# A decoder trunk on one core: the unpaired matrices of the input projection are chained, and TensorE keeps the order in which the kernel is written

## The chip, the cores and the metric

The kernel runs on one core of a Trainium2 chip. The metric is the device time of one execution in microseconds (us). Three runs of the kernel before took 1710.2 to 1712.84 us, with a median of 1712.13 us. About 0.2% (some 3.5 us) is what a measurement of this kernel can tell from no change.

## The reference, cut to what matters

One layer of a hybrid decoder on 1024 tokens of width 2048, in float32:

```
h = rms_norm(x, norm_gain)
q, k, v, g_attn, xr, g_rec = split(h @ w_in)          # 2048 -> 4*1024 + 2*1024
q, k = rope(q), rope(k)                               # 8 heads, 2 maps of 64 each
o = diff_attention(q, k, v, lam)                      # causal, softmax(1) - lam*softmax(2)
o = rms_norm(o, subln_gain) * 0.8 * silu(g_attn)
r = rg_lru(causal_conv(xr, conv_w, conv_b), ...)      # 8 blocks of 128 channels
r = r * silu(g_rec)
out = rms_norm(x + concat(o, r) @ w_out, final_gain)
```

## The kernel before, in words

Every product of two float32 matrices is split: an operand becomes a rounded high part and a rest, and three matmuls of 128x512 (high x high, high x rest, rest x high) stand for one. The high part is a cast on ACT, the rest a subtraction on DVE or POOL (`split`, L189 and L190; L193 is the helper for all other two-operand elementwise work).

**The input projection** works on *pairs*: two column blocks of 128 of `w_in`, over one half of the depth (8 of 16 tiles of 128) and all 1024 tokens. A pair is one 2x2 block product by a Strassen scheme, so it needs 7 products, numbered `pi` = 0 to 6, instead of 8. A product is one *group* of 12 matmuls (4 depth tiles x 3 split parts) into one PSUM bank. The weight operand of a product is formed by `prep` from the pair's four raw loads (`x["11"]`, `"12"`, `"21"`, `"22"`): products 0, 1, 4 and 5 take one tile as it lies, product 2 needs two additions first, products 3 and 6 one. The token operands (`OPS`, seven of them) are the same for all pairs of a stretch.

Four banks serve a pair: `al` for products 0 and 3, `de` for 1, `be` for 2 and 5, `ga` for 4 and 6 (`BANKS`). Products 3, 5 and 6 do not begin a bank: they add to what lies there. Between two products of a bank `post` reads it:

- after product 0: ACT copies `al` to `a1` (L546)
- after product 1: DVE adds `de` to `a1`: result 11
- after product 3: ACT copies `al` to `u2` (L552), then DVE adds `be` and `u2` to `u3`. Product 5 may write `be` only when that is done
- after product 4: DVE adds `ga` and `u3`: result 22. Product 6 may write `ga` only then
- after products 5 and 6: DVE adds `be` and `u2` (result 21), `ga` and `u2` (result 12)

In the rows all these bank reads of DVE are `L193 b<-pp`. `pp_78`, `pp_79`, `pp_80` and `pp_81` of the order are `al`, `be`, `ga` and `de`.

The projection has three stretches: 8 pairs of recurrent columns over the first depth half; 24 pairs (16 attention, 8 recurrent) over the second; 16 attention pairs over the first. A recurrent pair of the second stretch spawns `recurrent` when it is done (convolution, gates, scan: work for DVE, ACT and POOL), an attention pair of the third `rope` or `values`. The first two pairs and the last two of a stretch are *dual*: their groups alternate, each pair with banks of its own (in the third only the first two). All others are *single*: products 0 to 6 of one pair, then 0 to 6 of the next. The list `q` of (pair, product) holds that order.

The loop over `q` runs, per step: raw loads ahead, `prep` of the step three places on (`LEAD`), the 12 matmuls with a tick of `sl` after each three, and `post`. Side work lives in generators that `sl` resumes at ticks, so it lands between groups.

**What sets the order on the engines.** What the loop emits is not the final order. A scheduler that works with a cost model of its own puts each engine's instructions in order when the kernel is built; the place in the program is the priority. On the chip every engine then runs its list in that fixed order.

**The rest.** `rec_half` does the recurrent half of the output projection (groups of 24 matmuls at L1079 to L1081) and feeds the attention between them: scores of a block of 128 queries into PSUM `sw` (L870, L871), mask and maximum on DVE (L875, L878), exponentials on ACT (L882), the weighted difference on DVE (L885 to L890, result `wide`), transposes on PE (L997), their split (L1006 on ACT, L1007 on DVE), product with the values (L1019 to L1022), and once per half head a norm (`head_out`, L968 and L979 on PE). `att_half` does the other half of the output projection and the last norm.

Of the kernel before, what the change touches and what calls it, by code (L numbers as in the profile page):

```python
# [121 lines left out]
class Trunk:  # L122
# [419 lines left out]
    def post(self, pr, pi):  # L542
# [16 lines left out]
        elif pi == 6:  # L559
            self.result(pr, "12", b["ga"], pr.u2)  # L560
            self.rel(pr.u2)
            if pr.done:
                self.after.append(self.sl.spawn(pr.done(pr.c), 1))

    def projection(self):
        nc, sl = self.nc, self.sl
        recs = [(32 + 2 * n, 33 + 2 * n) for n in range(NR)]
# [11 lines left out]
        q, starts, ends, dualp = [], [], [], set()  # L579
        for si, (k, seg) in enumerate(segs):  # L580
            starts.append(len(q))
            groups = [seg[:2]] + [[p] for p in seg[2:-2]] + [seg[-2:]]
            if si == 2:
                groups[-1:] = [[p] for p in seg[-2:]]
            for g in groups:
                for i, p in enumerate(g):
                    p.s = i
                    if len(g) == 2:
                        dualp.add(p)
                q += [(p, pi) for pi in range(7) for p in g]  # L590
            ends.append(len(q))
        loads, parts, last = {}, {}, {}
        for i, (p, pi) in enumerate(q):
# [573 lines left out]
            self.rel(y)  # L1167

    def run(self):
        if True:  # L1170
            self.consts()
            self.projection()
            self.rec_half()
            self.att_half()
# [61 lines left out]
```

## Time and profile before

| | us |
|---|---|
| median of three runs | 1712.13 |
| the profiled execution | 1714.92 |
| its span, first to last instruction | 1713.1 |
| PE busy (matmul) | 1568.0 (92%) |
| DVE busy | 1281.2 (75%) |
| ACT busy | 815.5 (48%) |
| POOL busy | 629.7 (37%) |
| PE idle at the projection's matmuls (L659, four banks `pp`) | 102.8, of which 84.2 ended by DVE L193 |

The profile tells of each engine how long it was busy and, for an idle time, which instruction ended it. PE's row is to be read with care: a matmul counts as busy at the halved clock too, so the granted clock (mean 0.968 over the span) belongs beside it. The program has no single bound: the stretches of the projection (single pairs from 62 to 165, 239 to 732 and 806 to 1104 us), the attention with half of the output projection (1104 to 1542) and the rest (to 1713) have different ones.

### The profile page before, as it was taken

How to read it: one execution, taken by the hardware profiler on the slowest of the kernel's cores; microseconds unless marked ns; L12 is line 12 of the kernel's file. 1: busy time of each engine (PE TensorE's matmuls, PEld its weight loads, DVE VectorE, ACT ScalarE, POOL GpSimd, SP SyncE). 2: the span in 40 equal slices, each digit the busy share in tenths (PEclk: the TensorE clock that was granted, in tenths of full speed). 3: DMA queues.
4: the chain of work that ended last, by engine and by line, in shares of the span. 5: the costliest groups of instructions: out<-in, count | busy, mean ns of one | idle time of the engine just before them, and what ended most of it. 6: DMA issues, size and time to landing. Idle time of an engine off the chain costs nothing. (4 is left out here: it accounts for less than half of the span.)

```text
span 1713.1 us, 22261 instructions
## 1 busy us (share of the span) xinstructions
PE 1568.0 (92%) x7140; PEld 1268.1 (74%) x7140; DVE 1281.2 (75%) x2120; ACT 815.5 (48%) x1462; POOL 629.7 (37%) x486
## 2 busy tenths in 40 slices
PE   6888999898998988899899999989999999999997
PEld 4667877776776767687677778767777777778786
DVE  8966778977977887789999999857677777861412
ACT  6444535345355355553333333336555565663432
POOL 3474523323333242452223333324223322357370
PEclk9998999999999998999999999999999999999999
DMA  6665642332423323375766666878567655474642
GB/s 253 223 228 187 225 142 77 114 102 89 129 90 112 119 89 102 117 258 161 238 197 208 205 197 210 279 276 277 180 216 261 207 176 164 141 243 139 218 157 99
DMA packets 168277, 304.18 MB, mean 178 GB/s; under 512 B 19040, under 2 KB 21216, under 8 KB 168160
## 3 DMA queue, kind: packets, MB, share of 16 engines
q1 hardware_dynamic: 168160, 302.76, 53.3%
q8 instruction: 56, 0.92, 0.2%
q14 instruction: 61, 0.50, 0.1%
HBM read 206.22 MB, written 96.47 MB: 177 GB/s over the span
## 5 line engine op out<-in xcount | busy, mean ns | idle before, releaser
L659 PE MATMUL pp<-b,b 128*128 128x512 f32 x3612 | 888.5, 404 | 102.8 <-DVE b L193 84.2
L659 PEld LDWEIGHTS pp<-b,b 128*128 128x128 f32 x3612 | 700.3, 195 | 273.2 <-DVE b L193 98.8
L190 POOL TENSOR_TENSOR b<-b,b 128x512 fp32r<-128x512 f32 x288 | 449.3, 1574 | 636.8 <-ACT b L189 356.0
L189 ACT CAST b<-b 128x512 fp32r<-128x512 f32 x592 | 355.0, 619 | 549.9 <-DVE b L193 275.4
L190 DVE TENSOR_TENSOR b<-b,b 128x512 fp32r<-128x512 f32 x304 | 241.7, 807 | 66.4 <-ACT b L189 57.1
L193 DVE TENSOR_TENSOR b<-b,b 128x512 f32<-128x512 f32 x340 | 257.2, 771 | 16.8 <-POOL b L190 10.7
L1080 PE MATMUL pq<-b,b 128*128 128x512 f32 x512 | 204.2, 399 | 2.3 <-POOL b L190 1.6
L1081 PE MATMUL pq<-b,b 128*128 128x512 f32 x512 | 203.6, 398 | 2.8 <-DVE b L190 2.8
L1079 PE MATMUL pq<-b,b 128*128 128x512 f32 x512 | 203.2, 398 | 0.1
L193 DVE TENSOR_TENSOR b<-pp,b 128x512 f32<-128x512 f32 x215 | 147.0, 684 | 62.2 <-PE pp L659 50.0
L193 POOL TENSOR_TENSOR b<-b,b 128x512 f32<-128x512 f32 (+1 forms) x56 | 75.0, 1340 | 259.5 <-ACT b L733 92.9
L193 DVE TENSOR_TENSOR b<-pq,b 128x512 f32<-128x512 f32 x89 | 61.1, 687 | 116.3 <-PE pq L1081 111.0
L882 ACT ACTIVATE wide<-sw,mx 128x256 f32<-128x256 f32 (+7 forms) x128 | 93.9, 739 | 59.6 <-DVE mx L878 58.4
L1081 PEld LDWEIGHTS pq<-b,b 128*128 128x128 f32 x512 | 96.9, 190 | 20.1 <-DVE b L190 4.2
L875 DVE CUSTOM_DVE_ANT_0 sw<-sw,mask 128x256 f32<-128x256 f32 (+7 forms) x128 | 96.9, 763 | 19.6 <-PE sw L871 18.0
L1080 PEld LDWEIGHTS pq<-b,b 128*128 128x128 f32 x512 | 96.7, 189 | 19.3 <-POOL b L190 4.3
L1079 PEld LDWEIGHTS pq<-b,b 128*128 128x128 f32 x512 | 96.8, 189 | 16.4 <-ACT b L189 0.5
L193 DVE TENSOR_TENSOR b<-b,wide 128x512 f32<-128x512 f32 x120 | 99.6, 844 | 8.9 <-ACT wide L1149 8.3
L659 PE MATMUL pq<-b,b 128*128 128x512 f32 x420 | 103.5, 392 | 0.5 <-POOL b L190 0.5
L659 PEld LDWEIGHTS pq<-b,b 128*128 128x128 f32 x420 | 79.3, 189 | 17.5 <-POOL b L190 0.9
L1006 ACT CAST b<-pq 128x512 fp32r<-128x512 f32 (+1 forms) x80 | 43.5, 543 | 77.7 <-PE pq L997 74.7
L870 PE MATMUL sw<-b,b 128*128 128x512 f32 (+2 forms) x192 | 70.9, 372 | 7.4 <-ACT wide L882 7.0
(148 smaller groups left out, 1586.6 us busy)
## 6 DMA issues: line engine op xcount, KB each, us to landing
b<-w_in SPq DMA_DIRECT2D x192, 256.0 KB, 2.9
b<-w_out SPq DMA_DIRECT2D x128, 256.0 KB, 4.4
pt<-b SPq DMA_DIRECT2D x96, 256.0 KB, 2.8
b<-pt SPq DMA_DIRECT2D x96, 256.0 KB, 3.0
b<-fs SPq DMA_DIRECT2D x96, 256.0 KB, 4.4
b<-xt SPq DMA_DIRECT2D x72, 256.0 KB, 3.9
fs<-b SPq DMA_DIRECT2D x64, 256.0 KB, 3.4
b<-yd SPq DMA_DIRECT2D x32, 256.0 KB, 4.3
```

The lines of the kernel that those rows point to most:

```text
L189: self.nc.scalar.copy(hi.r, x)
L190: (eng or self.nc.vector).tensor_tensor(out=lo.r, in0=x, in1=hi.f, op=ALU.subtract)
L193: (eng or self.nc.vector).tensor_tensor(out=out, in0=a, in1=b, op=op)
L659: nc.tensor.matmul(acc, lhsT=a.r[:, s], rhs=b.r, start=FIRST[pi] and qq == 0 and j == 0, stop=qq == 3 and j == 2, skip_group_check=True)
L870: nc.tensor.matmul(o, lhsT=q[m].r[:, qs], rhs=kk, start=True, stop=False)
L875: nc.vector.tensor_tensor_reduce(out=s, in0=s, in1=self.mask[:, 896 - off:896 - off + cols], scale=1.0, scalar=NEG, op0=ALU.add, op1=ALU.m ...
L882: nc.scalar.activation(p[:, :cols], self.swide[m][:, :cols], AF.Exp, scale=QK ** -0.5, bias=mx[:, m:m + 1], accum_out=sm[:, m:m + 1])
L1006: nc.scalar.copy(wh.r[:, first:], self.tr[:, first:])
L1079: nc.tensor.matmul(acc, lhsT=mh.r[:, s], rhs=wh.r, start=kt == 0, stop=False)
L1080: nc.tensor.matmul(acc, lhsT=mh.r[:, s], rhs=wl.r, start=False, stop=False)
L1081: nc.tensor.matmul(acc, lhsT=ml.r[:, s], rhs=wh.r, start=False, stop=kt == 7)
```

## The change

Two things change.

`chained` builds the order of the single pairs of a stretch. The first single pair starts with its products 0, 1, 2. From then on, for each pair p and the next one n: p3, p4, n0, p5, n1, p6, n2, then n3, n4, and so on. Between p4 and p5, and between p5 and p6, stands a group of the next pair. Dual pairs stay as they were, and so do `prep`, `post`, the banks and LEAD.

`run` opens `manual_schedule` for PE: PE's instructions stand in the order in which the kernel emits them, everywhere in the program. The scheduler still orders the other engines.

```diff
+    def chained(self, pairs):
+        q = [(pairs[0], pi) for pi in range(3)]
+        for n, p in enumerate(pairs):
+            q += [(p, 3), (p, 4)]
+            for pi in (5, 6):
+                if p is not pairs[-1]:
+                    q.append((pairs[n + 1], pi - 5))
+                q.append((p, pi))
+            if p is not pairs[-1]:
+                q.append((pairs[n + 1], 2))
+        return q
...
             if si == 2:
                 groups[-1:] = [[p] for p in seg[-2:]]
+            single = [g[0] for g in groups if len(g) == 1]
             for g in groups:
                 for i, p in enumerate(g):
                     p.s = i
                     if len(g) == 2:
                         dualp.add(p)
-                q += [(p, pi) for pi in range(7) for p in g]
+                if len(g) == 2:
+                    q += [(p, pi) for pi in range(7) for p in g]
+                elif g[0] is single[0]:
+                    q += self.chained(single)
             ends.append(len(q))
...
     def run(self):
-        if True:
+        with self.tc.manual_schedule(engines={mybir.EngineType.PE}):
             self.consts()
```

Line numbers of the changed kernel are 18 higher behind the place where `q` is built: L659 becomes L677, L681 L699, L752 L770, L763 L781, L875 L893, L887 L905, L890 L908, L968 L986, L979 L997, L997 L1015, L1007 L1025, L1019 to L1022 L1037 to L1040, L1079 to L1081 L1097 to L1099. Up to `post` (L189, L193, L546, L552) they stay.

**DVE in the second stretch**, between two bank reads of a pair, before: the four rows that read `pp` are u3, result 22, result 21 and result 12 of one pair.

```order
L193 TENSOR_TENSOR b_676_2723<-pp1_79,b_675_2722 128x512
L763 SCALAR_TENSOR_TENSOR b_669_2682<-b_671_2684,b_656_2626 128x512
L193 TENSOR_TENSOR b_662_2663<-b_662_2663,b_657_2641 128x512
L193 TENSOR_TENSOR b_679_2745<-pp2_80,b_676_2723 128x512
L190 TENSOR_TENSOR b_688_2776<-b_665_2671,b_687_2775 128x512
L763 SCALAR_TENSOR_TENSOR b_670_2683<-b_672_2685,b_669_2682,b_662_2663 128x512
L193 TENSOR_TENSOR b_653_2616<-b_686_2772,b_653_2616 128x512
L193 TENSOR_TENSOR b_683_2767<-pp1_79,b_675_2722 128x512
L681 SCALAR_TENSOR_TENSOR b_607_2392<-b_694_2813,b_607_2392 128x512
L190 TENSOR_TENSOR b_693_2801<-b_653_2616,b_692_2800 128x512
L190 TENSOR_TENSOR b_698_2824<-b_686_2772,b_697_2823 128x512
```

The same engine and pair now: the rows that read `pp` are result 12 of the pair before, u3, result 22 and result 21.

```order
L193 TENSOR_TENSOR b_662_2662<-pp2_80,b_633_2521 128x512
L770 SCALAR_TENSOR_TENSOR b_661_2650<-b_661_2650,b_675_2721 128x512
L193 TENSOR_TENSOR b_672_2711<-pp1_79,b_671_2710 128x512
L193 TENSOR_TENSOR b_687_2772<-b_653_2612,b_654_2614 128x512
L193 TENSOR_TENSOR b_679_2741<-pp2_80,b_672_2711 128x512
L193 TENSOR_TENSOR b_653_2612<-b_653_2612,b_641_2556 128x512
L193 TENSOR_TENSOR b_641_2556<-b_687_2772,b_641_2556 128x512
L190 TENSOR_TENSOR b_684_2750<-b_604_2369,b_683_2749 128x512
L190 TENSOR_TENSOR b_689_2776<-b_653_2612,b_688_2775 128x512
L770 SCALAR_TENSOR_TENSOR b_667_2687<-b_667_2687,b_676_2722 128x512
L193 TENSOR_TENSOR b_666_2672<-b_666_2672,b_661_2650 128x512
L781 SCALAR_TENSOR_TENSOR b_675_2721<-b_677_2723,b_666_2672 128x512
```

The additions that form operands for products 2, 3 and 6 (two-operand L193 rows on `b` alone) moved from in front of u3 to behind it, in front of result 21.

**DVE in the attention**, at one query block, before: the mask of the next block (L875 on `sw`) stands in front of the weighted difference (L890) of this one.

```order
L1007 TENSOR_TENSOR b_2392_10808<-pq0_66,b_2391_10807 128x512
L887 SCALAR_TENSOR_TENSOR mx_2385_10768<-sm_2386_10769,nlam_735,mx_2385_10768 128x1
L875 ISA sw1_9462,mx_2397_10833<-sw1_9462,mask_93 128x768
L875 ISA mx_2397_10833 128x1
L890 SCALAR_TENSOR_TENSOR wide1_71<-wide3_73,mx_2385_10768,wide1_71 128x640
L1007 TENSOR_TENSOR b_2400_10844<-pq0_66,b_2399_10843 128x384
```

And now:

```order
L905 SCALAR_TENSOR_TENSOR mx_2385_10770<-sm_2386_10771,nlam_736,mx_2385_10770 128x1
L908 SCALAR_TENSOR_TENSOR wide1_71<-wide3_73,mx_2385_10770,wide1_71 128x640
L1025 TENSOR_TENSOR b_2392_10810<-pq0_66,b_2391_10809 128x512
L1025 TENSOR_TENSOR b_2400_10846<-pq0_66,b_2399_10845 128x384
L893 ISA sw0_9463,mx_2397_10835<-sw0_9463,mask_95 128x768
```

The weighted difference (now L908) stands in front of the next block's mask (now L893).

**PE at the end of the attention**, before: matmuls of `att_half` (into `pq2`) stand between the norm's two steps (L968 and, nine rows behind these, L979) of the last half head.

```order
L968 MATMUL pq1_67<-ones_84,b_2931_13721 128x1 x4
L1080 MATMUL pq2_68<-b_2851_13238,b_2936_13746 128x512
L1081 MATMUL pq2_68<-b_2850_13237,b_2937_13747 128x512
L1079 MATMUL pq2_68<-b_2892_13541,b_2939_13752 128x512
L1080 MATMUL pq2_68<-b_2893_13542,b_2939_13752 128x512
L1081 MATMUL pq2_68<-b_2892_13541,b_2940_13753 128x512
```

And now:

```order
L1037 MATMUL pq1_67<-b_2924_13696,b_2828_13135 128x256
L1039 MATMUL pq1_67<-b_2924_13696,b_2829_13137 128x256
L1040 MATMUL pq1_67<-b_2925_13697,b_2828_13135 128x256
L986 MATMUL pq1_67<-ones_86,b_2931_13723 128x1 x4
L997 MATMUL pq1_67<-ident_94,hs_2933_13732 128x128 x4
L1097 MATMUL pq2_68<-b_2850_13239,b_2936_13748 128x512
```

The last product with the values and the two steps of the norm follow each other directly; the matmuls of `att_half` begin behind them.

## Rows read from the trace of the kernel before

**Rows 1.** Busy time, clock (PEclk) and DMA of four stretches, us.

```profile
62.00:165.00 103.00, 85.52 (x339) 68.73 (x338) 67.75 (x76) 44.75 (x78) 64.39 (x44) 0.90 0.67 222
239.00:732.00 493.00, 435.86 (x1794) 351.90 (x1793) 401.94 (x515) 241.05 (x361) 164.75 (x117) 0.94 0.33 105
806.00:1104.00 298.00, 283.37 (x1242) 228.47 (x1241) 279.44 (x422) 107.60 (x188) 93.24 (x45) 0.99 0.65 213
1104.00:1542.00 438.00, 409.21 (x2248) 331.28 (x2247) 312.98 (x769) 251.35 (x513) 141.37 (x161) 0.98 0.65 218
```

**Rows 2.** PE's waits in these four stretches: us, times, longest.

```profile
PE pp L659 <- DVE b L193: 17.5, 4, 5.8
PE pp L659 <- DVE b L193: 57.1, 18, 6.4
PE pp L659 <- DVE b L193: 9.6, 11, 2.8
PE pq L997 <- DVE wide L890: 14.3, 12, 2.8
PE sw L870 <- ACT wide L882: 7.0, 10, 2.2
```

**Rows 3.** Timeline, PE: start, length, count, [idle before, releaser]; dual, then single pairs.

```profile
165.75 2.88 PE L659 MATMUL pq<-b,b 128*128 128x512 f32 x12
168.47 2.88 PE L659 MATMUL pp<-b,b 128*128 128x512 f32 x12
257.13 19.34 PE L659 MATMUL pp<-b,b 128*128 128x512 f32 x84 [2.35 <-DVE b L193]
400.20 6.46 PE L659 MATMUL pp<-b,b 128*128 128x512 f32 x15 [5.20 <-DVE b L193]
726.51 5.69 PE L659 MATMUL pp<-b,b 128*128 128x512 f32 x24 [0.41 <-DVE b L193]
```

**Rows 4.** Timeline ahead of the wait at 400.20: PE, then ACT.

```profile
385.77 9.23 PE L659 MATMUL pp<-b,b 128*128 128x512 f32 x40
...
398.32 0.62 ACT L189 CAST b<-b 128x512 fp32r<-128x512 f32 x1 [2.12 <-POOL b L193]
398.84 0.58 ACT L552 COPY b<-pp 128x512 f32<-128x512 f32 x1
```

**Rows 5.** Timeline of the same place: DVE, then POOL.

```profile
393.71 1.78 DVE L707 SCALAR_TENSOR_TENSOR b<-xp,vec,b 128x512 f32<-128x512 f32 x1
...
399.45 0.69 DVE L193 TENSOR_TENSOR b<-pp,b 128x512 f32<-128x512 f32 x1
...
393.18 3.44 POOL L190 TENSOR_TENSOR b<-b,b 128x512 fp32r<-128x512 f32 x2 [4.73 <-ACT b L189]
```

**Rows 6.** Timeline ahead of an earlier wait of PE: ACT.

```profile
324.65 0.62 ACT L189 CAST b<-b 128x512 fp32r<-128x512 f32 x1 [4.65 <-DVE b L193]
325.17 0.58 ACT L552 COPY b<-pp 128x512 f32<-128x512 f32 x1
```

**Rows 7.** Stretches right behind the waits at 257.13 and 400.20, columns as in Rows 1.

```profile
257.00:260.50 3.50, 3.37 (x15) 2.79 (x16) 3.50 (x6) 0.00 (x0) 0.00 (x0) 1.00 0.18 69
...
400.20:403.70 3.50, 3.50 (x8) 2.80 (x9) 3.45 (x6) 0.96 (x2) 0.00 (x0) 0.50 0.60 184
```

**Rows 8.** Timeline of a 1024-wide query block: last score, weighted difference, its transposes.

```profile
1265.41 0.39 PE L871 MATMUL sw<-b,b 128*128 128x512 f32 x1
...
1272.91 1.28 DVE L890 SCALAR_TENSOR_TENSOR wide<-wide,mx,wide 128x1024 f32<-128x1024 f32 x1
...
1274.34 0.49 PE L997 MATMUL pq<-ident,wide 128*128 128x128 f32 x3
```

**Rows 9.** End of the projection: PE, SP's queue, and issues with us to landing.

```profile
1098.54 5.75 PE L659 MATMUL pp<-b,b 128*128 128x512 f32 x24 [0.76 <-DVE b L193]
...
1110.45 3.83 SPq L176 DMA_DIRECT2D b<-fs  x6
...
b<-fs SPq DMA_DIRECT2D x12, 256.0 KB, 5.1
```

## The prediction

> **What bounds the kernel now.** I read the views in this order: busy time and clock by stretch, PE's waits by stretch, the timeline around the waits, and then the timelines of ACT, DVE and POOL just ahead of them.
>
> The share of PE busy says little here, so I set PE's work against its time. Twelve matmuls of a group start 2.72 us after the twelve before, 0.227 us each (168.47 less 165.75 [rows 3]). The 1794 matmuls of the single pairs from 239 to 732 us are then 407 us of work in 493 us [rows 1]. The 86 us that are missing have two parts. PE waits 57.1 us, in 18 waits that a DVE operation ends [rows 2]. The granted clock of 0.94 [rows 1] means that 12% of 493 us, 59 us, ran at 1.2 GHz instead of 2.4, and half of that, 29.6 us, is lost. In the stretch from 62 to 165 the same reckoning gives 17.5 us of waits [rows 2] and, at a clock of 0.90, 10.3 us [rows 1]. From 806 to 1104 DVE is busy 279.4 of 298 us [rows 1] and PE waits only 9.6 us for it [rows 2].
>
> The waits stand at one place. Before and behind a wait lie 84 matmuls, a whole pair (at 257.13 [rows 3]). Counted from the start of the single pairs, the wait always comes behind product 4: product 5 may not write `be` before u3 is formed. Between the end of product 3 and that point lies one group, 2.72 us. At 400.20 the steps can be followed: product 4 ends at 395.0, so product 3 had ended near 392.2 [rows 4]. ACT's copy of `al` should have started then, but it starts at 398.84, because ahead of it in ACT's queue a cast waited for POOL [rows 4]; DVE's addition follows at 399.45 [rows 5] and PE goes on at 400.20 [rows 3]. In another pair the cast ahead of the copy waited 4.65 us for a DVE addition that forms an operand [rows 6]. So PE is held by queues that are late, and one group is too little cover.
>
> **The change, part by part.** *The chain* neither adds nor removes an instruction of the projection. It moves distances. From product 3 to product 5 there are now two groups (4 and the next pair's 0), 5.44 us instead of 2.72; from 4 to 6 three instead of one. Paid for it is slack that lay unused: the `be` read after product 5 has two groups instead of three, the `ga` read after 6 two instead of four. One distance becomes as short as the old one: `al` is written by the next pair's product 0 one group after product 3, but that waits for ACT's copy alone, not for copy and addition. The 18 waits between 239 and 732 us run from 2.35 us (the first) to 0.41 (the last), with 5.20 among them [rows 3], 6.37 the longest [rows 2]. Less one group each, eleven are left over, 16.6 us in all: 40.5 us gained. The clock: behind the wait of 2.35 us it stays at 1.00, behind that of 5.20 it is 0.50 [rows 7]. Thirteen of the waits exceed 2.5 us, four of the rests come near that or over it, so of 29.6 us some 9 stay and 20 are gained. What comes late next is DVE itself: its 401.9 us [rows 1] would fill 93% of a stretch that is 60 us shorter, and from 806 to 1104, where it fills 94%, PE still loses 16 us or more (1242 matmuls of at most 0.227 us are 282 [rows 1]). I take 8 us back. Sum: **-52**, stretch at 441 us.
>
> From 62 to 165 the four waits of 17.5 us [rows 2], less one group each, leave 6.6 (gain 10.9), and about 6 of 10.3 us of slow clock go with them. Against it stands POOL, busy 64 of 103 us [rows 1], to which the new order gives the casts' rests of products 0, 5 and 1 in three steps in a row; I take 3 us for it. **-14.** From 806 to 1104 all waits are under one group, but DVE's 279.4 us are a floor near 285 [rows 1]; half of the 13 us above it and a little more: **-8**.
>
> *PE in the written order.* In the single pairs PE's list was already the written one, group by group, so nothing changes there beyond the chain. At the start (the first 60 us) the groups of the two dual pairs no longer interleave: **+2**, between 0 and 5, the work of nine matmuls that cannot slip ahead when the last operand comes. In the attention three things move. First, the products and transposes stand further from their sources, except one: between the last score matmul of the second block of a pair and the first transpose of it lay 7.3 to 8.9 us of PE's work and now lie 10.6, 6.2, 5.9 and 5.7 us, counted from the order with 0.227 us for 512 columns. Today that path takes 8.5 us in a 1024-wide block (from 1265.8 to 1274.34 [rows 8]), but then DVE did the next block's mask ahead of the weighted difference; now it stands behind, so a mask of some 1.2 us leaves the path. I expect some 2 us of waits at two of four pairs of blocks, 8 heads, 30 us, against 14.3 + 7.0 now [rows 2] and small ones that go: **0** to +10; I take +2. Second, at the entry the first scores stand behind 15 matmuls and a transpose, 3.8 us after the projection, but their loads are issued until 1114.3 and land 5.1 us later, 15 us after its end at 1104.3 [rows 9]; with the last `rope` now finishing three groups earlier, a wait between 0 and 11 us: **+6**. Third, at the end nothing of `att_half` fills the last half head's norm: some **+5** for two splits, two copies and a root. Together +15.
>
> Sum: -52 - 14 - 8 + 15 = -59. The profiled execution took 1714.9 us, 2.8 over the median; against the median of 1712.1 this gives **1653 us**.
>
> **A rule that speaks against it.** A DVE operation next to POOL's takes 1.78 us (at 393.71, with POOL busy from 393.18), one that finds POOL idle 0.69 (at 399.45) [rows 5]. The Trainium skill, "SBUF — State Buffer", section "Who interferes with whom", says that a DVE instruction with two SBUF inputs contends with a GpSimd instruction that reads SBUF, and that the loser blocks fully. The rows bear that out in kind. By that rule a shorter stretch pushes more of the two engines' work on top of each other; it is the third rival below.
>
> **The rivals.**
>
> *The wait moves to the copy.* If ACT's copy stays as late as at 398.84, product 0 of the next pair waits for it, one group behind product 3. Then each wait shrinks only by the addition and its hop, 0.75 us (from the copy's end at 399.4 [rows 4] to 400.20): 13 us over 18 waits, and the clock stays. Were every copy late like this, -13 - 3 - 4 in the three stretches; were half, the waits give (13 + 40) / 2 = 27 us and the clock some 6, so about -33 - 8 - 6. With +15 that is 1707 or 1680; I put the half, **1680**. For it: the copy was the late part in both pairs shown [rows 4, 6]. Against it: the operand additions on which such casts wait now stand behind u3 in DVE's list, not in front.
>
> *DVE and POOL block each other.* Each of POOL's 117 operations between 239 and 732 [rows 1] can stretch one of DVE's by 1.1 us. If half of them do so in addition, DVE needs 466 us, and at 94% the stretch stays at 493: 0 - 10 - 4 + 15, **1713**. Against it: the count of POOL's operations does not grow.
>
> *Slower: PE's list in the attention is too tight.* If the path from score to transpose keeps its 8.5 us, PE waits 2.3, 2.6 and 2.8 us in three of four pairs of blocks, 62 us over 8 heads. Sixteen of these exceed 2.5 us, each with 2.3 us of slow clock behind it (29.6 us over the 13 such waits of the second stretch), 37 us. Less the 21 us of today's waits that is +78, beside +13 for the other moves and -74: **1729**. It decides from about 8 us more per head than I take (61 us over 8 heads). For it: the measured 8.5 us. Against it: the new place of the mask.
>
> *The chain gives all.* No rest of a wait, no slow clock behind it, no loss at the entry: -86 + 8 - 22 - 14 + 8, **1606**.
>
> **How the numbers follow.** Forecast 1653: 0.55. Copy, 1680: 0.20. DVE and POOL, 1713: 0.06, spread over all three signs. Slower, 1729: 0.11. All, 1606: 0.08. About 0.2% (3.5 us) is what a measurement of this kernel can tell from no change. Faster: 0.55 + 0.20 + 0.08 + 0.02 = 0.85; within 0.2%: 0.03; slower 0.12. The range reaches from 1610 (bounds of the chain's gain) to 1710, so that it takes in the copy's case and leaves out most of the slower one.
>
> **What the profile after would show.** Right: PE's waits on DVE L193 between the single pairs fall from 57.1 to about 17 us, the clock there rises from 0.94 to about 0.98, the stretch takes about 441 us. The copy's case: PE waits on ACT L552, in front of the next pair's product 0. The third: DVE's mean per L193 and L190 row rises. The slower case: PE's waits on the weighted difference (now L908) grow from 14.3 to over 60 us. The entry: a PE wait on a DMA `b<-fs` in front of the first score. It would be wrong at its root if the single pairs lost their waits and the time stayed.

## The result, and the profile after

The changed kernel takes **1771.57 us** (median; 1768.21 to 1776.58), the kernel before beside it on the same chip 1712.49. The ratio is 1.0339, with a 95% interval of 1.0316 to 1.0363: slower by 3.4%, some 59 us. The forecast was 1653. The single pairs of the second stretch did get faster; the other parts together lost three times that gain.

The parts of the span, from the starts of the projection's matmuls in the profiled execution (start: the first single pair begins; duals: the four dual parts between the stretches; attention: up to the last norm step of `head_out`). The labels are those of the experiments below.

| us | start | 1st single | 2nd single | 3rd single | duals | attention | rest | span |
|---|---|---|---|---|---|---|---|---|
| before | 60.3 | 102.7 | 490.1 | 296.0 | 154.8 | 438.2 | 171.0 | 1713.1 |
| **after** | 62.2 | 104.9 | 463.9 | 318.8 | 155.3 | 475.0 | 186.3 | 1766.4 |
| e1_chain | 61.4 | 103.6 | 464.7 | 320.9 | 156.5 | 437.2 | 171.6 | 1715.8 |
| e2_written | 62.5 | 104.5 | 490.6 | 296.3 | 155.8 | 477.9 | 186.7 | 1774.2 |
| e3_written_out | 61.1 | 101.0 | 489.1 | 297.0 | 154.9 | 485.9 | 186.8 | 1775.8 |
| e4_swap | 64.0 | 98.7 | 448.9 | 310.2 | 160.0 | 432.6 | 171.7 | 1686.2 |
| e5_third_plain | 63.1 | 98.4 | 448.4 | 307.8 | 157.1 | 436.5 | 171.5 | 1682.7 |
| e6_pool_off | 62.6 | 97.7 | 447.5 | 286.0 | 160.6 | 441.6 | 173.3 | 1669.3 |
| e7_split_early | 61.4 | 101.7 | 486.6 | 296.7 | 154.8 | 464.0 | 187.8 | 1753.2 |
| e8_both_between | 64.5 | 102.1 | 457.9 | 306.5 | 158.0 | 439.0 | 172.3 | 1700.3 |
| e9_before_pool_off | 61.9 | 101.7 | 488.9 | 288.2 | 156.4 | 434.2 | 170.9 | 1702.2 |
| e10_pool_off_0_2 | 58.2 | 101.1 | 448.8 | 282.1 | 156.7 | 443.3 | 171.0 | 1661.2 |
| e11_pool_off_all | 59.2 | 97.8 | 420.4 | 285.4 | 157.4 | 436.3 | 171.2 | 1627.8 |
| e12_before_pool_off_all | 58.0 | 100.8 | 443.2 | 284.8 | 153.2 | 437.5 | 173.1 | 1650.5 |
| e13_chain_pool_off | 64.0 | 93.6 | 439.5 | 282.7 | 154.1 | 439.9 | 170.5 | 1644.3 |
| e14_best_free | 59.6 | 102.1 | 416.6 | 281.6 | 155.5 | 440.3 | 171.0 | 1626.8 |

So the change gains 26 us in the second stretch and loses 2 at the start, 2 in the first, 23 in the third, 37 in the attention and 15 in the rest: 53 us between the two profiled executions, where the medians differ by 59.

Busy time of five parts of the changed kernel, in the columns of [rows 1]:

```profile
62.00:167.00 105.00, 86.36 (x338) 68.80 (x337) 61.02 (x72) 44.26 (x78) 62.76 (x44) 0.89 0.65 206
243.00:707.00 464.00, 427.01 (x1782) 346.51 (x1781) 378.13 (x512) 239.69 (x358) 167.58 (x116) 0.95 0.34 111
786.00:1105.00 319.00, 288.45 (x1233) 231.95 (x1232) 296.58 (x423) 109.57 (x190) 80.14 (x48) 0.96 0.61 201
1105.00:1580.00 475.00, 399.82 (x2185) 330.99 (x2184) 312.99 (x767) 247.77 (x504) 131.99 (x155) 0.96 0.59 194
1580.00:1766.00 186.00, 176.37 (x771) 145.25 (x769) 47.22 (x81) 64.89 (x140) 90.60 (x71) 0.98 0.44 154
```

The rest of the kernel before, in the same columns:

```profile
1542.00:1713.00 171.00, 160.51 (x709) 132.28 (x707) 45.87 (x79) 61.80 (x133) 84.69 (x67) 0.98 0.45 153
```

Two things are to be read here. In the third stretch DVE is busy 296.6 us for 423 operations; before it was 279.4 for 422 [rows 1]. And 62 matmuls have moved from the attention (2248 before [rows 1], 2185 now) to the rest (709, then 771): at 0.227 us they are 14 us, nearly all of the 15 by which the rest is longer. Before, the output projection ran ahead in the attention, and some 62 of its last 768 matmuls found room there; now all 768 lie behind it.

PE's waits in the changed kernel (us in total, times, longest), in the second stretch, the third, and the attention; they answer to [rows 2]:

```profile
PE pp L677 <- ACT b L552: 30.1, 9, 4.4
PE pp L677 <- ACT b L546: 4.3, 1, 4.3
PE pp L677 <- DVE b L193: 2.2, 2, 2.0
...
PE pp L677 <- DVE b L193: 13.3, 6, 4.4
PE pp L677 <- ACT b L552: 9.9, 6, 2.3
PE pq L837 <- DVE b L193: 4.7, 1, 4.7
...
PE pq L1015 <- DVE b L1025: 23.5, 18, 2.9
PE pq L1015 <- DVE wide L908: 20.4, 16, 3.1
PE pq L997 <- DVE hs L994: 10.0, 11, 2.2
PE sw L888 <- ACT wide L900: 8.4, 11, 2.7
PE sw L888 <- DMA b<-fs: 7.5, 1, 7.5
PE sw L889 <- DMA b<-fs: 1.6, 2, 1.0
```

Of the 57.1 us on DVE L193 of the second stretch [rows 2] 2.2 are left, and 30.1 us on ACT's copy L552 stand in their place: nine waits, by PE's order all in front of a next pair's product 0. In the attention the weighted difference (L908) costs 20.4 us against 14.3 [rows 2], and three waits appear: transposes behind the split of the transposes before them (L1025, 23.5 us), the norm's second step (L994), and the first scores behind their loads. Before, the first of the three was small:

```profile
PE pq L997 <- DVE b L1007: 1.7, 4, 0.6
```

One of the nine waits, on PE, then ACT, then POOL, in the timeline of the changed kernel (start, length, count, idle before and releaser):

```profile
391.83 6.96 PE L677 MATMUL pp<-b,b 128*128 128x512 f32 x30
402.94 1.65 PE L677 MATMUL pp<-b,b 128*128 128x512 f32 x3 [4.15 <-ACT b L552]
...
401.27 1.14 ACT L189 CAST b<-b 128x512 fp32r<-128x512 f32 x2 [5.69 <-POOL b L193]
402.31 0.58 ACT L552 COPY b<-pp 128x512 f32<-128x512 f32 x1
...
396.70 1.74 POOL L190 TENSOR_TENSOR b<-b,b 128x512 fp32r<-128x512 f32 x1 [1.28 <-DVE b L193]
398.40 2.84 POOL L193 TENSOR_TENSOR b<-b,b 128x256 fp32r<-128x256 f32 x2
```

It is the picture of [rows 4] with another releaser. ACT stands idle 5.69 us at the head of its queue, on a cast that waits for POOL; POOL is late because a rest (L190) stood in front; the copy comes right behind the casts, and PE goes on 0.63 us after the copy has started. The addition u3, on which PE waited before, is no longer what ends last. The place is typical: in seven of the nine waits, 28.4 of the 30.1 us, ACT had last stood idle on a cast that waited for POOL's L193.

One wait of the attention, PE, ACT and DVE:

```profile
1311.11 0.55 PE L1015 MATMUL pq<-ident,wide 128*128 128x128 f32 x3 [1.11 <-DVE wide L908]
...
1314.42 0.55 PE L1015 MATMUL pq<-ident,wide 128*128 128x128 f32 x3 [1.38 <-DVE b L1025]
...
1311.22 0.80 ACT L900 ACTIVATE wide<-sw,mx 128x640 f32<-128x640 f32 x1 [3.79 <-DVE mx L896]
...
1312.01 0.79 ACT L900 ACTIVATE wide<-sw,mx 128x640 f32<-128x640 f32 x1
...
1312.78 0.58 ACT L1024 CAST b<-pq 128x512 fp32r<-128x512 f32 x1
...
1313.08 0.69 DVE L193 TENSOR_TENSOR b<-pq,b 128x512 f32<-128x512 f32 x1
1313.69 0.68 DVE L1025 TENSOR_TENSOR b<-pq,b 128x512 fp32r<-128x512 f32 x1
```

All transposes go through one bank. The first ones end near 1311.7, but their split starts at 1312.78, behind the two exponentials of the next block, and its second step on DVE behind an addition. PE has six matmuls in its list, 1.4 us, between the two sets of transposes; the way through ACT and DVE took 2.7 us.

### The profile page after: what moved, and what is told of

Same layout as the page of the kernel before. It is cut to its first block, busy times and chain, and to the rows that moved or that the text cites. A ratio compares the mean times of both kernels' runs of the same rounds, so it can differ in the third digit from the quotient of the medians.

```text
span 1766.4 us, 22315 instructions
## 1 busy us (share of the span) xinstructions
PE 1575.8 (89%) x7140; PEld 1281.5 (73%) x7140; DVE 1274.5 (72%) x2120; ACT 817.9 (46%) x1462; POOL 614.9 (35%) x486
## 5 line engine op out<-in xcount | busy, mean ns | idle before, releaser
L677 PE MATMUL pp<-b,b 128*128 128x512 f32 x3612 | 886.6, 404 | 96.6 <-ACT b L552 49.4
L677 PEld LDWEIGHTS pp<-b,b 128*128 128x128 f32 x3612 | 701.3, 196 | 264.9 <-ACT b L552 57.3
L190 POOL TENSOR_TENSOR b<-b,b 128x512 fp32r<-128x512 f32 x288 | 429.5, 1505 | 794.8 <-ACT b L189 470.0
L189 ACT CAST b<-b 128x512 fp32r<-128x512 f32 x592 | 354.5, 620 | 559.3 <-DVE b L193 199.4
L190 DVE TENSOR_TENSOR b<-b,b 128x512 fp32r<-128x512 f32 x304 | 232.5, 778 | 73.8 <-ACT b L189 54.1
L193 DVE TENSOR_TENSOR b<-b,b 128x512 f32<-128x512 f32 x340 | 266.1, 798 | 23.9 <-POOL wide L193 9.9
L1097 PE MATMUL pq<-b,b 128*128 128x512 f32 x512 | 211.9, 414 | 0.0
L1099 PE MATMUL pq<-b,b 128*128 128x512 f32 x512 | 203.2, 397 | 0.0
L193 DVE TENSOR_TENSOR b<-pp,b 128x512 f32<-128x512 f32 x215 | 146.1, 680 | 41.9 <-ACT b L552 22.0
L193 DVE TENSOR_TENSOR b<-pq,b 128x512 f32<-128x512 f32 x89 | 61.0, 686 | 124.9 <-PE pq L1099 124.5
L900 ACT ACTIVATE wide<-sw,mx 128x256 f32<-128x256 f32 (+7 forms) x128 | 93.8, 737 | 102.3 <-DVE mx L896 97.8
L193 POOL TENSOR_TENSOR b<-b,b 128x512 f32<-128x512 f32 (+1 forms) x56 | 81.4, 1456 | 112.5 <-DVE b L1000 39.4
L1099 PEld LDWEIGHTS pq<-b,b 128*128 128x128 f32 x512 | 98.0, 191 | 21.8
L193 DVE TENSOR_TENSOR b<-b,wide 128x512 f32<-128x512 f32 x120 | 106.8, 904 | 8.9 <-ACT wide L1167 8.3
L893 DVE CUSTOM_DVE_ANT_0 sw<-sw,mask 128x256 f32<-128x256 f32 (+7 forms) x128 | 95.3, 773 | 21.3 <-PE sw L889 20.2
L1098 PEld LDWEIGHTS pq<-b,b 128*128 128x128 f32 x512 | 98.5, 192 | 15.9 <-POOL b L190 1.4
L1097 PEld LDWEIGHTS pq<-b,b 128*128 128x128 f32 x512 | 98.5, 192 | 14.4
L677 PE MATMUL pq<-b,b 128*128 128x512 f32 x420 | 101.9, 391 | 1.1 <-POOL b L190 0.7
L677 PEld LDWEIGHTS pq<-b,b 128*128 128x128 f32 x420 | 78.7, 188 | 19.1 <-POOL b L190 1.1
L1015 PE MATMUL pq<-ident,wide 128*128 128x128 f32 x288 | 51.7, 290 | 45.0 <-DVE b L1025 23.5
```

The lines of the kernel that those rows point to most:

```text
L189: self.nc.scalar.copy(hi.r, x)
L190: (eng or self.nc.vector).tensor_tensor(out=lo.r, in0=x, in1=hi.f, op=ALU.subtract)
L193: (eng or self.nc.vector).tensor_tensor(out=out, in0=a, in1=b, op=op)
L677: nc.tensor.matmul(acc, lhsT=a.r[:, s], rhs=b.r, start=FIRST[pi] and qq == 0 and j == 0, stop=qq == 3 and j == 2, skip_group_check=True)
L893: nc.vector.tensor_tensor_reduce(out=s, in0=s, in1=self.mask[:, 896 - off:896 - off + cols], scale=1.0, scalar=NEG, op0=ALU.add, op1=ALU.m ...
L900: nc.scalar.activation(p[:, :cols], self.swide[m][:, :cols], AF.Exp, scale=QK ** -0.5, bias=mx[:, m:m + 1], accum_out=sm[:, m:m + 1])
```

## The experiments

**Theory A** after the traces: the two halves of the change are independent. The chain moves PE's wait to ACT's copy and saves what is left; the written order costs some 50 us in the attention and behind it. Four runs undo or exchange one part each.

**e1_chain**: the chain alone.

```diff
-        with self.tc.manual_schedule(engines={mybir.EngineType.PE}):
-            self.consts()
+        self.consts()
...
```

> The chained order of the projection alone; PE's order is left to the scheduler, as in the kernel before. Theory A (the two parts add up: in the projection the chain saves 26 us in the second stretch and gives 23 back in the third, and the written order costs 37 us in the attention and 15 behind it): about 1714 us, second stretch 464, third 319, the attention back at 438. Rival B (the third stretch is longer because of the written order there, where PE's side work, the transposes of `values`, may not slip ahead of a waiting group): third stretch near 296, time near 1690. Rival C (the chain leaves DVE behind, and this is what makes the attention long): the attention stays near 475, time near 1765.

Measured: 1716.11 us, ratio 1.0012 (0.9992 to 1.0031). The chain alone is worth nothing that can be measured: 465 us in the second stretch, 321 in the third, and the attention is back at 437. Theory A holds; B (third stretch at 296) and C (attention near 475) fall. Its waits in the second stretch and in the attention:

```profile
PE pp L677 <- ACT b L552: 32.7, 9, 4.4
...
PE pq L1015 <- DVE wide L908: 12.8, 10, 2.8
PE sw L888 <- ACT wide L900: 8.0, 10, 2.0
...
PE pq L1015 <- DVE b L1025: 2.0, 5, 0.6
```

**e2_written**: the written order of PE in the whole program, the pairs as before (the diff of the change without `chained`).

> The written order of PE in the whole program alone; the pairs of the projection as before. Theory A: 1712 + 2 (start) + 37 + 15 = about 1766 us, with PE's waits on L1007 (split of transposes) and on the weighted difference L890 near 24 and 20 us in the attention, and the third stretch at 298. Rival B: third stretch about 315, time near 1785. Rival C: attention near 445, time near 1735.

Measured: 1773.48 us, 1.0362 (1.0335 to 1.0389). Attention 478, rest 187, stretches as before: theory A, a few us more than it said. The whole loss of the changed kernel, and a little more, is there without any chain.

**e3_written_out**: the written order around the last two phases alone.

```diff
+        self.consts()
+        self.projection()
         with self.tc.manual_schedule(engines={mybir.EngineType.PE}):
-            self.consts()
-            self.projection()
             self.rec_half()
             self.att_half()
```

> The written order of PE in `rec_half` and `att_half` alone, behind a projection as before. Theory A: the same loss as with the written order everywhere, less the 2 us at the start: about 1764 us; attention near 475, the rest near 186. Rival C: near 1735. Rival D (what the written order costs is at the seam and in the projection): near 1715.

Measured: 1774.89 us, 1.0365 (1.0346 to 1.0385). The loss sits in `rec_half` and `att_half`; D falls. Its waits in the attention are those of the changed kernel (L997, L1007 and L979 are L1015, L1025 and L997 there):

```profile
PE pq L997 <- DVE b L1007: 26.8, 18, 2.9
PE pq L997 <- DVE wide L890: 20.5, 15, 3.1
PE pq L979 <- DVE hs L976: 10.5, 11, 2.2
...
PE sw L870 <- DMA b<-fs: 8.0, 1, 8.0
```

**e4_swap**: the chain with more room for the copy, PE written in the projection alone.

```diff
-        q = [(pairs[0], pi) for pi in range(3)]
+        q = [(pairs[0], pi) for pi in (1, 0, 2)]
...
-                    q.append((pairs[n + 1], pi - 5))
+                    q.append((pairs[n + 1], 6 - pi))
```

> The chain with the next pair's products 1 and 0 exchanged (p3, p4, n1, p5, n0, p6, n2), so that `al` has three groups between product 3 and the next product 0 instead of one, and its result 11 formed when both are done; raw tile 12 is loaded three steps earlier. PE keeps the written order in the projection alone. Theory A: PE's waits on the copy L552 (49 us) go nearly all, with some clock behind them: second stretch 425 to 440, third 300 to 310, attention 438, time about 1665. Rival E (DVE is the bound; the wait only shows at whichever product is nearest): waits of the same size reappear on DVE L193 at products 5, 6 or 1, second stretch near 464, time near 1713.

Measured: 1692.28 us, 0.988 (0.9859 to 0.9901): the first version that beats the kernel before. The waits on the copy are gone, as A said. Most of them come back on u3 at product 5, as E said: 24.7 us in the second stretch, where 30.1 us on the copy went. The stretch is 449, neither A's 425 to 440 nor E's 464, and the third 310. Of the 15 us that the second stretch gained, half are waits of PE (37.0 to 29.4 us in all), half PE's busy time (427.0 to 419.6 us), with the clock up from 0.95 to 0.97.

```profile
PE pp L680 <- DVE b L194: 25.1, 11, 4.0
```

**The third stretch.** In the versions with a chain it was longer than 296 us so far. In the trace an addition or subtraction of DVE with both operands in SBUF takes 0.68 us where POOL is idle and 1.16 us on the mean, 1.79 at most, where it meets an operation of POOL (after, third stretch: 237 of the first kind, 84 of the second). With one operand in PSUM it takes 0.68 us either way (18 of these meet POOL). Taking 0.68 from the longer ones, DVE loses 40 us there, against 21 before. Next come two runs on that.

**e5_third_plain**: as e4_swap, third stretch in the order of before.

```diff
+                elif si == 2:
+                    q += [(p, pi) for pi in range(7) for p in g]
                 elif g[0] is single[0]:
```

> As e4_swap (products 1 and 0 of the next pair exchanged in the chain, PE in the written order in the projection alone), but the third stretch keeps the order of the kernel before, pair by pair. Theory A (in the third stretch the chain itself is the loss: it puts DVE's additions beside POOL's rests): third stretch back from 310 to about 296, the operations of DVE with two operands in SBUF beside POOL back from some 1.09 to 0.84 us, time about 1678 us. Rival G (the third stretch is long because the shorter second one leaves side work to it): third stretch stays near 310, time near 1692.

Measured: 1685.9 us, 0.9838 (0.9799 to 0.9877). A fails here: the third stretch is 308 us, not 296, in the very order of products that took 296. DVE loses 29 us beside POOL, in the kernel before 21. That is rival G's time, but its mechanism is not seen: DVE does 416 operations there and POOL 45, before 422 and 45 [rows 1]. The chain in the third stretch is thus not the cause by itself. With both operands in SBUF, 90 operations of DVE meet POOL here and 91 before, but each loses 0.30 us on the mean instead of 0.21; why is not shown.

**e6_pool_off**: as e4_swap, but in the third stretch POOL forms no rests.

```diff
-        eng = self.nc.gpsimd if pi in POOL_LO else self.nc.vector
+        eng = self.nc.gpsimd if pi in POOL_LO and (pr.k or not pr.done) else self.nc.vector
```

> As e4_swap with the chain in all three stretches, but in the third the rests of products 0, 1 and 5 go from POOL to DVE. DVE gets some 40 operations of 0.68 us more (27 us). Theory A (beside POOL DVE loses 41 us there: 99 operations of 1.09 us against 0.68 alone): DVE's busy time in the third stretch falls from 295 to about 282, the stretch from 310 to about 297, time about 1679 us. Rival H (the longer operations beside POOL fill time in which DVE would have idled): DVE's busy time is a bound, and the stretch becomes 27 us longer, about 337, time near 1719.

Measured: 1667.83 us, 0.9727 (0.9703 to 0.9752). The third stretch falls from 310 to 286 us, below A's 297: DVE, the busiest engine besides PE, gets 33 operations more and is busy 276 us instead of 295, so H falls. The two-operand groups of DVE in the third stretch, in e4_swap (columns: busy us, mean ns, idle before):

```profile
L194 DVE TENSOR_TENSOR b<-b,b 128x512 f32<-128x512 f32 x142 | 117.1, 841 | 13.9 <-issue 9.0 <-DMA vs<-b 4.3 <-DVE b L191 0.2
L194 DVE TENSOR_TENSOR b<-b,wide 128x512 f32<-128x512 f32 x90 | 71.7, 816 | 0.4
...
L194 DVE TENSOR_TENSOR b<-pp,b 128x512 f32<-128x512 f32 x70 | 47.5, 679 | 0.8 <-PE pp L680 0.8
```

and in e6_pool_off:

```profile
L194 DVE TENSOR_TENSOR b<-b,b 128x512 f32<-128x512 f32 x141 | 94.0, 690 | 0.0
...
L194 DVE TENSOR_TENSOR b<-b,wide 128x512 f32<-128x512 f32 x88 | 59.2, 695 | 0.0
L194 DVE TENSOR_TENSOR b<-pp,b 128x512 f32<-128x512 f32 x69 | 47.4, 686 | 3.3 <-ACT b L555 1.7 <-PE pp L680 1.2
```

The rows with two operands in SBUF fall from 841 and 816 ns to 690 and 695; the row that reads a bank (`pp`) has nearly the same mean in both, 679 and 686. The Trainium skill, "SBUF — State Buffer", section "Who interferes with whom", says that a DVE instruction with two SBUF inputs contends with a GpSimd instruction that reads SBUF, and that one with at most one SBUF input, outside the modes that use both ports, does not; the means agree.

**e7_split_early**: as e3_written_out, the split of the transposes emitted three matmuls earlier.

```diff
                         self.turn(ws, k2, first)
-                        yield 1
                         w = self.unturn(first)
+                        yield 1
                         if k2 == nkb // 2 - 1:
```

> As e3_written_out (projection as before, PE in the written order in `rec_half` and `att_half`), PE's list unchanged; ACT's copy and DVE's subtraction of a transposed block are emitted three matmuls earlier, right behind the transposes, so that they come ahead of other work in ACT's and DVE's lists. Theory A (the transposes into the single bank come too close behind the last ones, and what is queued ahead of the split on DVE decides): PE's waits on the split L1007 fall from 27 to 10 to 15 us, time from 1775 to about 1757 to 1765. Rival I (the distance on PE alone decides, some 2 us against copy, subtraction and their hops): waits stay above 20 us and the time near 1775.

Measured: 1755.21 us, 1.0237 (1.0212 to 1.0262): 20 us back with the same list of PE: the waits on the split fall from 26.8 to 11.2 us. Theory A; rival I falls. What stays is the distance of PE's list and the other waits:

```profile
PE pq L997 <- DVE wide L890: 19.1, 16, 3.1
PE pq L979 <- DVE hs L976: 12.0, 12, 2.2
PE pq L997 <- DVE b L1007: 11.2, 15, 2.7
```

**e8_both_between**: as e5_third_plain, with p3, p4, n1, n0, p5, p6, n2.

```diff
             q += [(p, 3), (p, 4)]
-            for pi in (5, 6):
-                if p is not pairs[-1]:
-                    q.append((pairs[n + 1], 6 - pi))
-                q.append((p, pi))
+            if p is not pairs[-1]:
+                q += [(pairs[n + 1], 1), (pairs[n + 1], 0)]
+            q += [(p, 5), (p, 6)]
```

> As e5_third_plain, but in the first two stretches the next pair's products 1 and 0 both stand between 4 and 5 (p3, p4, n1, n0, p5, p6, n2): three groups from product 3 to 5 instead of two, two from 3 to the next 0 instead of three, and one instead of two from 5 to the next 2, which writes `be` when result 21 has been read. Theory A (the late part is copy and addition behind product 3): of the 26 us at product 5 some 10 stay, some waits come at the next product 0 and 2, second stretch 449 to about 440, time about 8 us below e5_third_plain. Rival E (DVE's queue is late whatever it has to do): the waits move to the next product 2, behind result 21, and the time is that of e5_third_plain or above.

Measured: 1701.61 us, 0.9921 (0.9898 to 0.9944), 16 us above e5_third_plain: rival E, and A fails. The waits in the second stretch:

```profile
PE pp L681 <- DVE b L194: 23.8, 12, 4.6
PE pp L681 <- ACT b L555: 13.1, 6, 2.8
```

By PE's order, the third group empties product 5: 0.2 us of waits stay there, of 24.2 in e5_third_plain. But 23.6 of the 23.8 us on DVE now stand in front of the next pair's product 2, which waits for result 21, as E said: DVE's queue is late, and the wait moves to the product that has the shorter distance. The copy, with one group less than in e4_swap, is waited for again. In this queue of ACT two groups for it are too few, three were enough.

**e9_before_pool_off**: the kernel before with the one line of e6_pool_off.

> The kernel before, with one change: in the third stretch the rests of products 0, 1 and 5 go from POOL to DVE, as in e6_pool_off. Theory A (an operation moved costs DVE 0.60 us, the distance between two starts, and gives back what DVE lost beside POOL): before, DVE loses 20 us in the third stretch beside POOL, not 41, so 42 moved operations cost 25 us and give back 16 or so: DVE 279 to 288 us busy, third stretch 296 to 300, time 1713 to 1717. Rival K (POOL's rests hold the products themselves, whatever the order): third stretch about 286 as in e6_pool_off, time about 1703.

Measured: 1704.01 us, 0.9946 (0.9921 to 0.9971), third stretch 288: rival K, not A. DVE had 20 us to win back by my sum and 25 to pay, and the stretch still fell by 8. Its busy time did not change (279.9 us, 279.4 before [rows 1]); what fell are PE's waits for its results, from 9.6 us [rows 2] to 4.2, and DVE's own waits for POOL's rests, 10.1 us in eight waits before and none now.

**e10_pool_off_0_2** and **e11_pool_off_all**: rests on DVE in the first and third stretch (and no written order at all), or in all three.

```diff
-        eng = self.nc.gpsimd if pi in POOL_LO else self.nc.vector
+        eng = self.nc.gpsimd if pi in POOL_LO and pr.k else self.nc.vector
```

```diff
-POOL_LO = (0, 1, 5)
+POOL_LO = ()
```

> As e6_pool_off, but the rests go to DVE in the first stretch too, and PE's order is left to the scheduler in the whole program. Theory A (18 to 22 us lost beside POOL in the first stretch, over 44 operations of POOL: 0.45 us for each, less than the 0.60 us that one costs DVE): the single pairs of the first stretch stay at 98 us or get up to 5 longer, the start is 1 to 2 us shorter: about 1666 to 1672 us. Rival K: the first stretch falls to about 90, time about 1658.

Measured: 1659.96 us, 0.968 (0.9652 to 0.9708); the first stretch is 101 us, no shorter: A. The time is 6 us below A's range; the start, the dual parts and the third stretch are some 4 us shorter each than in e6_pool_off.

> As e6_pool_off, but the rests of products 0, 1 and 5 go to DVE in all three stretches. Theory A: in the second stretch DVE loses 50 us beside 116 operations of POOL, 0.43 us for each; 60 operations moved cost 36 us and give back some 26: DVE 377 to about 387 us busy, second stretch 447 to 457, time 1668 to 1680. Rival K (the casts on ACT and the products wait for POOL's rests, not for DVE): second stretch about 435, time about 1655.

Measured: 1629.11 us, 0.9504 (0.9476 to 0.9533). A fails, and K's 435 is not low enough: the second stretch falls from 449 us (e4_swap) to 420. Its window and PE's waits in it:

```profile
233.00:654.00 421.00, 409.00 (x1784) 333.52 (x1783) 371.05 (x567) 236.97 (x358) 79.19 (x54) 1.00 0.37 122
```

```profile
PE pp L680 <- DVE b L194: 6.6, 5, 1.5
```

DVE does 567 operations instead of 505 and is busy 371 us instead of 378; the clock stands at 1.00. The sum of what an operation costs and gives back comes out near zero, near A's +10, but the stretch was not bound by that sum: PE's waits fell from 29.4 to 12.0 us. That POOL had been a slow link in front of the casts, as K has it, is not shown by this.

**e12_before_pool_off_all** and **e13_chain_pool_off**: the same line (`POOL_LO = ()`) in the kernel before, and in the chain as it was written in the change with PE free behind the projection.

> The kernel before, with one change: the rests of products 0, 1 and 5 are formed by DVE in all three stretches; no chain, PE's order left to the scheduler. Theory A (one group between product 3 and 5 is too little cover whenever a queue is late, and POOL makes the queues late: each cure takes a part): the 59 us of waits at product 5 in the second stretch fall to 15 to 30, stretch 489 to about 445, third 288, time about 1660. Rival L (the chain is worth nothing, POOL's rests are all of it): second stretch about 420, time about 1632. Rival M (without the chain the wait stays): second stretch about 485, time about 1700.

Measured: 1652.04 us, 0.9662 (0.9627 to 0.9697). Theory A: the waits at product 5 halve, from 56.7 us before to 28.0, and half stays. L and M fall.

> The chain as it was written in the change (the next pair's products 0 and 1 not exchanged), PE in the written order in the projection alone, and the rests of products 0, 1 and 5 on DVE in all three stretches. Theory A (POOL's queue makes the casts late that stand in front of the copy of `al`): PE's waits on the copy L552 in the second stretch fall from 30 to under 8 us, stretch 464 to about 423, time about 1632 to 1638. Rival N (one group between product 3 and the next product 0 is too short for the copy anyhow): waits on L552 of 15 us or more, stretch about 440, time about 1650.

Measured: 1648.76 us, 0.9636 (0.9604 to 0.9669). Rival N: the copy is still waited for. PE's waits in the second stretch, e12 and then e13:

```profile
PE pp L659 <- DVE b L193: 28.0, 16, 3.1
```

```profile
PE pp L677 <- ACT b L552: 22.3, 12, 3.5
```

One of the twelve, PE, ACT and POOL in e13, at the place of the timeline above:

```profile
376.97 1.21 PE L677 MATMUL pp<-b,b 128*128 128x512 f32 x4 [3.06 <-ACT b L552]
...
375.30 1.14 ACT L189 CAST b<-b 128x512 fp32r<-128x512 f32 x2 [5.10 <-POOL b L193]
376.34 0.58 ACT L552 COPY b<-pp 128x512 f32<-128x512 f32 x1
...
370.28 4.99 POOL L193 TENSOR_TENSOR b<-b,b 128x256 fp32r<-128x256 f32 x2 [13.51 <-ACT b L734]
```

No rest stands in front of POOL's work here, POOL had been idle for 13.5 us, and ACT still waits 5.1 us for it: this is the work that `recurrent` leaves on POOL. In seven of the twelve waits, 17.8 of the 22.3 us, ACT had last stood idle on a cast that waited for POOL's L193. So the run does not separate N's reason from A's: the rests are gone, POOL as a link in front of the copy is not.

With POOL's rests out of the way the chain as written moves 28.0 us of waits on u3 to 22.3 us on the copy, and the intervals of the two kernels overlap. With products 1 and 0 exchanged (e11) the second stretch is 19 us shorter again.

**e14_best_free**: as e11_pool_off_all, PE's order left to the scheduler everywhere.

> As e11_pool_off_all (products exchanged, rests on DVE everywhere), but PE's order is left to the scheduler in the whole program. Theory A: the single pairs are the same, the start gains 0 to 2 us: 1627 to 1631 us. Rival: the scheduler lets side work in front of waiting groups and loses some us in the second stretch, about 1637.

Measured: 1624.02 us, 0.9479 (0.9441 to 0.9517), 3 us below A's range. The intervals of e11 and e14 overlap; either is some 5% faster than the kernel before. The rival falls.

## Why the prediction was wrong, point by point

The forecast change and the one between the profiled executions differ by 112 us (-59 against +53). The third stretch has 31 of them, the attention with its entry 29, the second stretch 26, the first 16 and the end 10.

**The second stretch** (-52 forecast, -26 measured). The step that failed stands in one sentence of the part on the chain: one distance becomes as short as the old one, "but that waits for ACT's copy alone, not for copy and addition". The addition with its hop is 0.75 us; the copy was the late part, and it was late by its queue. In the seven pairs where ACT stood idle for POOL the wait gave back little more than that addition instead of a whole group: 34.2 us before, 28.4 now, 0.8 us each. The other waits nearly went. In all 57.1 us became 37 (30.1 + 4.3 + 2.2 and 0.4 elsewhere), not 16.6, and the clock went from 0.94 to 0.95, not to 0.98. This was the copy's rival, in place and in size: 27 us of waits and 6 of clock there, 20 and 6 here. e4_swap, e8 and e13 show the cause by its distance: waits on the copy at one and at two groups, none to speak of at three. But e4_swap and e8 show as well that DVE's queue came next, at whichever product had the shortest distance.

The sentence that spoke against that rival, that the operand additions now stand behind u3 on DVE, held and did not matter: the cast in the timeline above waits for POOL's part of `recurrent`.

Two counts in the prediction are off by one: twelve of the 18 waits exceed 2.5 us, not thirteen, and the last, 0.41 us, stands in front of product 6. Neither moves the sum.

**The first stretch** (-14 forecast, +2 measured) is the same error for one half: 17.5 us of waits [rows 2], now 9.3 on the copy and 9.3 on DVE. Of the latter 8.3 us stand at product 5, where two groups were too little for u3 as well.

**The third stretch** (-8 forecast, +23 measured). The forecast took DVE's 279.4 us [rows 1] as a floor that the change cannot move. It moved by 17 us with the same operations. Of the third rival the mechanism was right here (two operands in SBUF beside POOL), and its reason against, that the count of POOL's operations does not grow, was no reason: fewer of DVE's operations with both operands in SBUF meet POOL now (84 against 91), and each loses 0.48 us on the mean instead of 0.21. An operation of POOL cost DVE 0.47 us before (21 us over 45) and 0.83 now (40 over 48), in place of the priced 1.1. That price compared two different operations, of which the shorter reads a bank: L707 by itself takes 0.75 us where POOL is idle. In the second stretch, where the rival expected the loss, DVE's busy time fell, from 401.9 us [rows 1] to 378.1 for nearly the same operations.

The forecast also called the slack behind product 6 unused. In the third stretch it was used: of the 13.3 us on DVE 8.9 stand in front of product 4, which now writes `ga` two groups after product 6 instead of four, and 9.9 us are on the copy. What the 23 us owe to the chain alone is not settled all the same: e5 has the old order there and 308 us. That POOL's rests cost the stretch its time is shown: 310 to 286 us without them.

**The start** (+2) is +2.

**The attention in the written order** (+2 taken, 0 to +10 given). I priced one distance, from score to transpose, and found it long enough; that one came out at 20.4 against 14.3 us. The distance that broke is another in the same code, from a set of transposes through the split to the next set into the single bank (1.7 us before, 23.5 now), and the norm's two steps within each half head (10.0), which I had priced for the last half head only. The waits rise from 21.3 us [rows 2] and a few small ones to 71.4 (the six rows above), the clock falls from 0.98 to 0.96. The slower rival had the right sign. It gave the written order +91 us where start, attention and rest lost 54, by a mechanism that took no more than 6 us. e2 and e3 show that this loss is the written order's alone; e7 shows the split's path, 22 of the 48 us that the attention lost in e3.

**The entry** (+6, 0 to 11 given): 7.5 + 1.6 us of waits on `b<-fs`, inside the bounds of the term.

**The end** (+5 forecast, +15 measured). The norm of the last half head was priced; the 62 matmuls of `att_half` that before found room inside the attention were not: 14 us.

**The range** left out the sum of two losses. The copy's rival has -33 - 8 - 6 in the projection, the slower one +78 + 13 for the written order; both at once give 1712 - 47 + 91 = 1756. Each had a chance by itself and the pair had none, though e1 and e2 show that the two have nothing to do with each other.

## What to carry to other kernels

When a reordering lengthens one distance, write down the distance of every other pair of writer and reader on the same banks, and price each with the lateness of the queue it goes through, not with the length of the operation. A group moved in front of one wait can show the next one in the same queue, as in e8_both_between. An order by hand on one engine needs the same list for every bank that is used in turn, and loses the fill that a scheduler put into waits. An engine that helps out can cost more than it takes over: here moving the rests from POOL to the busier DVE made each version faster in which it was tried in the second or third stretch, the kernel before by 60 us. In the first stretch the move gained nothing (e10).

## What the runs showed of the hardware that I had not expected

Taking POOL's rests from it cost DVE nothing. In the second stretch 62 operations more, some 40 us at 0.68, left its busy time at 371 us (e11), against 378 (e4_swap). Most of that is covered by the operations that meet POOL: they lose 17 us instead of 51. The Trainium skill, "Perfetto Trace Analysis", section "Optimizing Scalar/DVE Operations", says that offloading between GpSimd and DVE might not help, since they share a read port; the runs agree and put a number to it: -60 us of 1712 for taking it back (e12). How much of the second stretch's 28 us came from shorter operations and how much from casts that no longer stood behind POOL's queue is not told apart by these runs: ACT's casts waited 36.0 us for POOL's L194 there in e4_swap, 24.5 in e11, but for the same line (L193) 29.5 before and 41.5 in e12, so that wait does not fall wherever the time does.
